# Low-rank products of the RWKV preparations in plain fp32, from a weight tile and an input tile of their own

## The chip, the cores and the metric

The kernel runs on one core of a Trainium2 chip. The metric is device time in microseconds (us) of one execution, the median of the runs shown. Five engines work side by side, each with an instruction queue in order: PE (TensorE, matrix multiply), DVE (VectorE), ACT (ScalarE), POOL (GpSimd) and SP, which here only issues DMA transfers. PEld is PE's loading of weights.

## The reference

One layer of a hybrid decoder on 576 tokens (64 of 8 sampled sequences, 512 of one prompt), width 1024: a joint input projection, a Mamba-2 branch, an RWKV-7 branch, an output projection, a SwiGLU and an embedding gate. The change touches one spot of the RWKV branch, where two low-rank products make the decay and the in-context rate of every token and channel:

```python
u = rw + (prev - rw) * w['shift_mu']          # token shift of the projected columns
r, k, v, w_lo, a_lo, g_lo = jnp.split(u, RWKV_SPLITS, axis=-1)   # w_lo, a_lo: 64 columns each
w_log = -jax.nn.softplus(-(w['w0'] + jnp.tanh(w_lo) @ w['w2']).astype(f32)) - 0.5
decay = jnp.exp(-jnp.exp(w_log))
a = jax.nn.sigmoid((w['a0'] + a_lo @ w['a2']).astype(f32))
```

## The kernel before

Channels lie on the 128 partitions and the 576 tokens along the free axis, in two halves of 288 columns (`HV`). Nearly every matrix product is done to fp32 precision from split operands: a tensor is cast to a high part (type fp32r, on ACT) and the rest is subtracted into a low part (on DVE or POOL), and `mm3` adds up three matmuls, high x high, high x low, low x high. A second helper, `fsum`, multiplies plain fp32 tiles with one matmul instruction a half; before the change it is used for the bonus term only.

Weights stream in blocks of 128 x 512 (`wsplit`, L206 to L213): SP loads a block into `raw` (three buffers), ACT casts it to `whi`, and DVE or POOL makes `wlo`. `whi` and `wlo` have two buffers each, and a buffer is free again when the last matmul that reads it is done. `linear` makes one output tile of 128 channels from two such blocks; a block is 24 matmuls for 576 tokens. A counter, `flip`, is raised by every `split` and `wsplit`; where no engine is named, an odd number gives the low part to POOL and an even one to DVE.

The program begins with the input's normalisation, the projected tile of the low-rank inputs (`ul`: 64 rows for the decay, through tanh, and 64 for the rate) and the tile of the gate. `ul` stays in use until the last quarter; `split` makes `ulh` and `ull` from it, which live in buffers of their own, while `ul` itself is a slot of the shared ring `s`. Meanwhile `norm_x` makes the eight normalised input tiles and their splits `xhi` and `xlo`, and the first projection tiles are computed from the unnormalised input `xu`.

Then the 16 RWKV heads are worked through in four quarters of 256 channels. A quarter has its six projection tiles, the preparation (`prep`: the low-rank products, decays, keys), the Gram matrices (`gram`), the bonus, a triangular solve on DVE (`solve`, `combine`) and a chain over nine chunks of tokens (`chain`). Between these, at places written out by hand (`FP`, `FILL`), `fill` puts further projection tiles (convolution and z) to give PE work. Behind the last quarter come the Mamba-2 branch, the output projection, the SwiGLU with its seven-product scheme (L1424) and the embedding gate.

In a preparation, `wsplit` loads and splits the quarter's low-rank weights `wl` (128 rows: 64 for the decay, 64 for the rate) into one of the two pairs `whi`, `wlo`, and `lora` makes four products from them, two per channel tile, each six matmuls long and read out by a tanh on ACT. `fill_at` may put a projection tile ahead of the first product, between the channel tiles and behind the second (`FP` gives one tile at each of these places in quarters 0 to 2, none in quarter 3).

The order of the instructions on each engine's queue isn't that of the program text. A planner takes instructions by their place in the text as their priority, and by when its own model has them ready and their buffers free, and writes one fixed order per engine.

Of the kernel before, what the change touches and what calls it, by code (L numbers as in the profile page):

```python
# [8 lines left out]
F32 = mybir.dt.float32  # L9
# [7 lines left out]
P = 128  # L17
D = 1024
NT = 576
# [22 lines left out]
RW_LORA, RW_GATE = 24, 25  # L42
# [33 lines left out]
def hybrid_step(ctx, tc, A):  # L76
    nc = tc.nc
# [10 lines left out]
    def nm(s):  # L88
        uid[0] += 1
        return f"{s}_{uid[0]}"  # L90

    def act(out, in_, func=AF.Copy, scale=1.0, bias=0.0):
        return S.activation(out, in_, func, bias=bias, scale=scale)  # L93
# [13 lines left out]
    def lin_ps(off=224):  # L107
        return lin_bank()[:, off:off + NT]
# [19 lines left out]
    def par(name, i=0):  # L128
        at, _ = PV[name]
        return pv[:, at + i:at + i + 1]  # L130
# [54 lines left out]
    def below(lo, src, hi, eng):  # L185

        if eng == "D":
            act(lo, src, scale=-1.0)
            G.dma_start(lo, src, accum_op=ALU.add)
        else:  # L190
            eng.tensor_tensor(lo, src, hi.bitcast(F32), ALU.subtract)  # L191

    def split(src, pool, tags, shape, lo_eng=None, hi=None, lo=None, hi_eng=None, **kw):
        hi = hi if hi is not None else pool.tile(shape, F32R, tag=tags[0], name=nm(tags[0]), **kw)
        lo = lo if lo is not None else pool.tile(shape, F32R, tag=tags[1], name=nm(tags[1]), **kw)
        if hi_eng:
            hi_eng.tensor_copy(hi[:], src)
        else:
            act(hi[:], src)
        flip[0] += 1  # L200
        below(lo[:], src, hi[:], lo_eng or (G if flip[0] % 2 else V))
        return hi, lo

    def wsplit(src, n, hi=None, lo=None):
        raw = wp.tile([P, 512], F32, tag="raw", name=nm("raw"), bufs=3)
        nc.sync.dma_start(raw[:, 0:n], src)  # L206
        if hi is None:
            hi = wp.tile([P, 512], F32R, tag="whi", name=nm("whi"))
            lo = wp.tile([P, 512], F32R, tag="wlo", name=nm("wlo"))
        act(hi[:, 0:n], raw[:, 0:n])  # L210
        flip[0] += 1
        eng = only[0] or (G if flip[0] % 2 else V)
        eng.tensor_tensor(lo[:, 0:n], raw[:, 0:n], hi[:, 0:n].bitcast(F32), ALU.subtract)  # L213
        return hi, lo
# [11 lines left out]
    def mm3(ps, whi, wlo, xhi, xlo, first, last, halves=None):  # L226
        for a, b in halves or HV:
            T.matmul(ps[:, a:b], whi, xhi[:, a:b], start=first, stop=False)  # L228
            T.matmul(ps[:, a:b], whi, xlo[:, a:b], start=False, stop=False)  # L229
            T.matmul(ps[:, a:b], wlo, xhi[:, a:b], start=False, stop=last)  # L230
# [20 lines left out]
    def fsum(ps, w, x):  # L251
        for a, b in HV:
            T.matmul(ps[:, a:b], w, x[:, a:b], start=True, stop=True)
# [3 lines left out]
    sp = mix.enter_context(tc.tile_pool(name="sp", bufs=1, side="right"))  # L257
# [3 lines left out]
    se = early_.enter_context(tc.tile_pool(name="se", bufs=1))  # L261
# [17 lines left out]
    def cb_ps():  # L279
        return bank(sq_, "cb", 1)  # L280

    def slot(name, shape=None, dt=F32):
        return se.tile(shape or [P, NT], dt, tag="s", name=nm(name), bufs=NSLOT)

    def cslot(name, shape=None, dt=F32):
        return sp.tile(shape or [P, NT], dt, tag="cv", name=nm(name), bufs=3)
# [73 lines left out]
            X.append(split(xr[k][:], xp, ("xhi", "xlo"), [P, NT]))  # L360


    def shifted(c, early=False, odd=False):
        ps = lin_ps()
        if early:
            linear(XU, ps)
            u = se.tile([P, NT], F32, tag="ar", name=nm("u"), bufs=2)
            V.tensor_tensor(u[:], ps, r0[:], ALU.mult)
            ps = u[:]
        else:  # L370
            linear(X, ps)
        t = sp.tile([P, NT], F32, tag="vo", name=nm("rw"), bufs=2) if odd else slot("rw")
        act(t[:], ps, AF.Identity, scale=omu[:, c:c + 1])
        mu = par("shift_mu", c)
        V.scalar_tensor_tensor(t[:, 0:65:8], sst[:, c, :], mu, t[:, 0:65:8], ALU.mult, ALU.add)
        V.scalar_tensor_tensor(t[:, ND + 1:NT], ps[:, ND:NT - 1], mu, t[:, ND + 1:NT], ALU.mult, ALU.add)
        t8, p8 = (a[:, 0:ND].rearrange("p (b t) -> p b t", b=8) for a in (t, ps))
        V.scalar_tensor_tensor(t8[:, :, 1:8], p8[:, :, 0:7], mu, t8[:, :, 1:8], ALU.mult, ALU.add)
        act(sho[:, c, 0:8], ps[:, 7:64:8])
        act(sho[:, c, 8:9], ps[:, NT - 1:NT])  # L380
        return t
# [50 lines left out]
        V.scalar_tensor_tensor(x[:], x[:], 0.0, e[:], ALU.max, ALU.add)  # L432
        nc.sync.dma_start(dt_d[:], x[:])

    ul = shifted(RW_LORA, True)
    act(ul[0:64, :], ul[0:64, :], AF.Tanh)
    UL = split(ul[:], se, ("ulh", "ull"), [P, NT], bufs=1)

    def gate_in():
        ug = shifted(RW_GATE, True)  # L440
# [50 lines left out]
    def fill_at(s, i):  # L491
        fill(FP[s.q][i])
# [43 lines left out]
    def prep(s):  # L536
        q = s.q
        mid = q in (1, 2)
        s.AR = (se if mid else sp).tile([P, 2, 9, 64], F32, tag="ar" if mid else "arz", name=nm("ar"), bufs=1 + mid)
        s.G = (se, sp)[q % 2].tile([P, 9, 2, 2, 2, 64], F32, tag=f"G{q % 2}", name=nm("G"))  # L540
        s.PC = sp.tile([P, 2, 16], F32, tag="pc", name=nm("pc"), bufs=2)
        s.BK, s.kn = [], []
        wl = wsplit(A["wl2"][:, q * 512:q * 512 + 512], 512)

        def lora(rows, jj, bias):
            ps = lin_ps()
            c = slice((2 * rows + jj) * P, (2 * rows + jj) * P + P)
            mm3(ps, wl[0][:, c], wl[1][:, c], UL[0], UL[1], True, True)
            t = slot("lo")
            act(t[:], ps, AF.Tanh, scale=0.5, bias=bias)  # L550
            return t

        st = cb_ps()
        for jj in jj2:
            j = 2 * q + jj
            sq = slot("sqk")
            act(sq[:], s.k[jj][:], AF.Square, scale=par("k_k", j))
            token_sums(st, jj, sq)
        fill_at(s, 0)
        rn = inv_norm(st, "rn", 1.0, 0.0)  # L560
        for jj in jj2:
            j = 2 * q + jj
            k, r, v = s.k[jj], s.r[jj], s.v[jj]
            ip = lora(0, jj, hw[:, j:j + 1])
            act(ip[:], ip[:], AF.Identity, scale=0.5, bias=eps_t[:, 2:3])
            a = lora(1, jj, hw[:, 8 + j:9 + j])
            fill_at(s, 1 + 2 * jj)
            V.tensor_tensor_scan(ip[:], rmask[:], ip[:], 0.0, ALU.mult, ALU.add)
            pb = slot("pb", [P, NT + 1])
            act(pb[:, 1:NT + 1], ip[:], AF.Exp, scale=-C_DECAY)  # L570
            act(ip[:], ip[:], AF.Exp, scale=C_DECAY)
            V.tensor_tensor(s.AR[:, jj], g9(r[:]), g9(pb[:, 1:NT + 1]), ALU.mult)
            for e in range(2):
                act(s.G[H[e], :, jj, 1, e], s.AR[H[e], jj])
            G.tensor_copy(s.PC[:, jj, 0:8], pb[:, 8:65:8])
            G.tensor_copy(s.PC[:, jj, 8:16], pb[:, 128:NT + 1:64])
            G.memset(pb[:, 0:65:8], 1.0)
            G.memset(pb[:, 128:NT:64], 1.0)
            kk = slot("kk")
            for a0, b0, ps in by_channel(rn, jj, cb_ps, ""):  # L580
                V.scalar_tensor_tensor(kk[:, a0:b0], k[:, a0:b0], par("k_k", j), ps, ALU.mult, ALU.mult)
            bk = (se, sp)[q % 2].tile([P, 9, 2, 64], F32, tag=f"bk{q % 2}", name=nm("bk"), bufs=2)
            V.tensor_tensor(pb[:, 0:NT], kk[:], pb[:, 0:NT], ALU.mult)
            for e in range(2):
                act(s.G[H[e], :, jj, 0, e], g9(pb[H[e], 0:NT]))
            V.scalar_tensor_tensor(kk[:], a[:], 1.0, kk[:], ALU.add, ALU.mult)
            act(a[:], a[:], AF.Identity, scale=hka[:, j:j + 1], bias=hka[:, 8 + j:9 + j])
            V.tensor_tensor(a[:], a[:], k[:], ALU.mult)
            for e in range(2):
                h = H[e]  # L590
                V.scalar_tensor_tensor(bk[h, :, e, :], g9(kk[h, :]), 0.5, g9(ip[h, :]), ALU.mult, ALU.mult)
                G.tensor_tensor(bk[h, :, 1 - e, :], g9(a[h, :]), g9(ip[h, :]), ALU.mult)
            s.kn.append(a)
            fill_at(s, 2 + 2 * jj)
            s.BK.append(bk)
# [667 lines left out]
    for what in SEQ:  # L1263
# [7 lines left out]
        elif what == "y":  # L1271
            for j in range(6):
                t = cslot("yl")
                nc.sync.dma_start(t[:], yr_d[j][:])
                YR.append(split(t[:], xp, ("xhi", "xlo"), [P, NT], lo_eng=G))
        else:
            ps = lin_ps()
            linear(YR[0:6], ps)
            t = cslot("pr")
# [21 lines left out]
    for c in range(8):  # L1301
        ps = lin_ps()
# [59 lines left out]
    for f in range(3):  # L1362
        ps = lin_ps()
# [18 lines left out]
    for k in range(4):  # L1382
        xa, xb, t = ft("xa"), ft("xb"), ft("tt")
# [13 lines left out]
    for f in range(3, 4):  # L1397
        ps = lin_ps()
# [135 lines left out]
    for a, b in ((0, 320), (320, NT)):  # L1534
# [18 lines left out]
        for c in range(8):  # L1553
# [5 lines left out]
            ps = lin_bank()[:, 0:n]  # L1559
# [8 lines left out]
            t = ft("pg")[:, 0:n]  # L1568
# [8 lines left out]
        ps = rstd_by_token(acc, 1.0 / D, 0, n)  # L1577
# [150 lines left out]
```

## Time and profile before

| | |
|---|---|
| median of 3 runs | 1332.21 us (1329.48 to 1340.11) |
| the profiled execution | 1330.78 us, its span 1328.8 us |
| PE busy | 1225.6 us, 92% of the span |
| DVE, ACT, POOL busy | 887.1, 631.1, 611.6 us |
| mean granted PE clock | 0.95 |

A row of the timeline gives start, duration, engine, line, operation, tiles written and read, shapes, count, and in brackets the time the engine stood idle before it and what ended that. A row of a group gives count, then busy time and mean duration, then idle time before. Matmuls overlap in the records, so the time that one takes of PE is the distance between starts and not its duration. PE's granted clock is 1.00 or 0.50 in any short stretch.

### The profile page before, as it was taken

How to read it: one execution, taken by the hardware profiler on the slowest of the kernel's cores; microseconds unless marked ns; L12 is line 12 of the kernel's file. 1: busy time of each engine (PE TensorE's matmuls, PEld its weight loads, DVE VectorE, ACT ScalarE, POOL GpSimd, SP SyncE). 2: the span in 40 equal slices, each digit the busy share in tenths (PEclk: the TensorE clock that was granted, in tenths of full speed). 3: DMA queues.
4: the chain of work that ended last, by engine and by line, in shares of the span. 5: the costliest groups of instructions: out<-in, count | busy, mean ns of one | idle time of the engine just before them, and what ended most of it. 6: DMA issues, size and time to landing. Idle time of an engine off the chain costs nothing. (4 is left out here: it accounts for less than half of the span.)

```text
span 1328.8 us, 26626 instructions
## 1 busy us (share of the span) xinstructions
PE 1225.6 (92%) x10429; PEld 1127.1 (85%) x10429; DVE 887.1 (67%) x1570; ACT 631.1 (47%) x1274; POOL 611.6 (46%) x583
## 2 busy tenths in 40 slices
PE   6897999999989978899989988999999999999997
PEld 5786897889968966787869868899899999999996
DVE  6648666887696886953456567868895148883464
ACT  6565436534654373343434464455553225553363
POOL 5416513642365135122455655646465345655642
PEclk9898899899978979889989989999999999999998
DMA  5322242234232313262454542253333224424322
GB/s 166 122 69 72 78 116 67 86 96 121 72 110 74 100 52 87 95 200 88 140 187 140 176 151 65 72 169 106 96 107 89 87 76 114 125 57 135 100 88 72
DMA packets 96765, 140.29 MB, mean 106 GB/s; under 512 B 34961, under 2 KB 39313, under 8 KB 96641
## 3 DMA queue, kind: packets, MB, share of 16 engines
q1 hardware_dynamic: 93760, 133.36, 32.8%
q0 software_dynamic: 2304, 4.72, 2.0%
q8 instruction: 82, 1.34, 0.4%
q10 hardware_dynamic: 576, 0.52, 0.1%
q14 instruction: 43, 0.34, 0.1%
HBM read 106.10 MB, written 27.75 MB: 101 GB/s over the span
## 5 line engine op out<-in xcount | busy, mean ns | idle before, releaser
L213 POOL TENSOR_TENSOR wlo<-raw,whi 128x512 fp32r<-128x512 f32 (+1 forms) x92 | 125.4, 1363 | 307.9 <-ACT whi L93 230.3
L228 PE MATMUL lin<-xhi,whi 128*128 128x288 f32 (+1 forms) x784 | 243.0, 311 | 2.9 <-ACT whi L93 2.1
L230 PE MATMUL lin<-xhi,wlo 128*128 128x288 f32 (+1 forms) x784 | 241.2, 308 | 2.2 <-POOL wlo L213 2.2
L229 PE MATMUL lin<-xlo,whi 128*128 128x288 f32 (+1 forms) x784 | 240.8, 307 | 0.9 <-POOL xlo L191 0.9
L93 ACT ACTIVATE whi<-raw 128x512 fp32r<-128x512 f32 (+1 forms) x200 | 123.2, 616 | 213.3 <-PE lin L241 94.9
L228 PEld LDWEIGHTS lin<-xhi,whi 128*128 128x128 f32 (+1 forms) x784 | 150.5, 192 | 9.8 <-ACT whi L93 2.6
L229 PEld LDWEIGHTS lin<-xlo,whi 128*128 128x128 f32 (+1 forms) x784 | 150.3, 192 | 6.2 <-POOL xlo L191 2.1
L230 PEld LDWEIGHTS lin<-xhi,wlo 128*128 128x128 f32 (+1 forms) x784 | 150.3, 192 | 6.0 <-POOL wlo L213 2.8
L213 DVE TENSOR_TENSOR wlo<-raw,whi 128x512 fp32r<-128x512 f32 (+1 forms) x108 | 83.5, 774 | 73.5 <-PE lin L241 37.7
L1424 PE MATMUL lin<-T,wh 128*128 128x288 f32 x576 | 87.3, 296 | 2.6 <-ACT e L93 2.2
L1424 PEld LDWEIGHTS lin<-T,wh 128*128 128x128 f32 x576 | 80.2, 190 | 3.3 <-ACT e L93 2.4
L93 ACT ACTIVATE wh<-raw 128x512 fp32r<-128x512 f32 x72 | 45.1, 629 | 53.9 <-PE lin L1424 37.1
L191 POOL TENSOR_TENSOR wl<-raw,wh 128x512 fp32r<-128x512 f32 x36 | 57.1, 1586 | 13.1 <-PE lin L1424 7.5
L191 DVE TENSOR_TENSOR wl<-sw,wh 128x512 fp32r<-128x512 f32 x54 | 50.8, 940 | 8.6 <-ACT wh L93 4.5
L241 PE MATMUL lin<-ah,whi 128*128 128x288 f32 x352 | 54.7, 294 | 0.0
L241 PE MATMUL lin<-al,whi 128*128 128x288 f32 x352 | 54.4, 295 | 0.0
L241 PE MATMUL lin<-ah,wlo 128*128 128x288 f32 x352 | 54.2, 295 | 0.0
L681 DVE TENSOR_TENSOR tmp<-L,Tt 72x30 f32<-72x30 f32 (+14 forms) x120 | 51.4, 429 | 3.2
L1424 PE MATMUL lin<-T,wl 128*128 128x288 f32 x288 | 50.2, 299 | 0.0
L241 PEld LDWEIGHTS lin<-ah,whi 128*128 128x128 f32 x352 | 49.3, 188 | 0.0
L241 PEld LDWEIGHTS lin<-al,whi 128*128 128x128 f32 x352 | 49.2, 188 | 0.0
L241 PEld LDWEIGHTS lin<-ah,wlo 128*128 128x128 f32 x352 | 49.2, 188 | 0.0
(432 smaller groups left out, 3259.2 us busy)
## 6 DMA issues: line engine op xcount, KB each, us to landing
raw<-wts SPq DMA_DIRECT2D x271, 256.0 KB, 2.6
S<-s_wkv SPq DMA_DIRECT2D x8, 512.0 KB, 5.1
hd<-s_ssm SPq DMA_DIRECT2D x8, 512.0 KB, 3.5
o_ssm_s<-hd SPq DMA_DIRECT2D x8, 512.0 KB, 2.9
xbc_d<-E SPq DMA_DIRECT2D x12, 288.0 KB, 2.1
x<-xT SPq DMA_DIRECT2D x8, 288.0 KB
gate_d<-g SPq DMA_DIRECT2D x8, 288.0 KB, 2.5
bv_d<-rw SPq DMA_DIRECT2D x8, 288.0 KB
```

The costliest lines, as they stand in the source:

```text
L93: return S.activation(out, in_, func, bias=bias, scale=scale)
L191: eng.tensor_tensor(lo, src, hi.bitcast(F32), ALU.subtract)
L213: eng.tensor_tensor(lo[:, 0:n], raw[:, 0:n], hi[:, 0:n].bitcast(F32), ALU.subtract)
L228: T.matmul(ps[:, a:b], whi, xhi[:, a:b], start=first, stop=False)
L229: T.matmul(ps[:, a:b], whi, xlo[:, a:b], start=False, stop=False)
L230: T.matmul(ps[:, a:b], wlo, xhi[:, a:b], start=False, stop=last)
L241: T.matmul(ps[:, a:e], (hi, lo)[p][:, i * P:(i + 1) * P], xs[k + i][q][:, a:e], start=n == k + i == 0, stop=n == 2 and k + i == nk - 1, sk ...
L681: V.tensor_tensor(o, L[:, jx:jx + 1, jx + 1:32].to_broadcast([NB, jx, n]), Tt[:, 0:jx, jx:jx + 1].to_broadcast([NB, jx, n]), ALU.mult)
L1424: T.matmul(ps, (hi, lo)[p][:, k * P:(k + 1) * P], OPS[n][k][q], start=first and p == q == k == 0, stop=p == 1 and k == 3, skip_group_check ...
```

## The change

The low-rank input `ul` gets a buffer of its own of fp32 (in place of `ulh`; `ull` is gone) and isn't split. Each quarter's weights are loaded by SP straight into a tile `wl` of their own (one buffer) and aren't split either. The products are made by `fsum` instead of `mm3`. So the counter `flip` is raised five times less: once before `norm_x` and once in each preparation.

```diff
-    def shifted(c, early=False, odd=False):
+    def shifted(c, early=False, odd=False, home=None):
...
-        t = sp.tile([P, NT], F32, tag="vo", name=nm("rw"), bufs=2) if odd else slot("rw")
+        t = home or (sp.tile([P, NT], F32, tag="vo", name=nm("rw"), bufs=2) if odd else slot("rw"))
...
-    ul = shifted(RW_LORA, True)
+    ul = shifted(RW_LORA, True, home=se.tile([P, NT], F32, tag="ulh", name="ul"))
     act(ul[0:64, :], ul[0:64, :], AF.Tanh)
-    UL = split(ul[:], se, ("ulh", "ull"), [P, NT], bufs=1)
+    UL = ul
...
-        wl = wsplit(A["wl2"][:, q * 512:q * 512 + 512], 512)
+        wl = sp.tile([P, 512], F32, tag="wl", name=nm("wl"), bufs=1)
+        nc.sync.dma_start(wl[:], A["wl2"][:, q * 512:q * 512 + 512])
...
-            mm3(ps, wl[0][:, c], wl[1][:, c], UL[0], UL[1], True, True)
+            fsum(ps, wl[:, c], UL)
```

## The prediction

> **What bounds the kernel now.** I read the page's first parts for the engines, then stages of the span by windows, then the records of the products that change, then PE's waits around them.
>
> ```profile
> span 1328.8 us, 26626 instructions
> PE 1225.6 (92%) x10429; PEld 1127.1 (85%) x10429; DVE 887.1 (67%) x1570; ACT 631.1 (47%) x1274; POOL 611.6 (46%) x583
> 0.00:70.00 70.00, 51.65 (x344) 48.13 (x345) 45.67 (x66) 40.76 (x72) 31.49 (x52) 0.95 0.44 143
> 70.00:110.00 40.00, 36.26 (x285) 34.81 (x284) 22.09 (x36) 26.30 (x47) 11.84 (x13) 0.96 0.20 61
> 110.00:180.00 70.00, 59.59 (x463) 54.50 (x462) 56.20 (x110) 30.22 (x60) 34.46 (x46) 0.85 0.27 79
> 325.00:440.00 115.00, 106.51 (x1050) 93.06 (x1049) 86.19 (x166) 60.03 (x137) 51.67 (x60) 0.90 0.29 89
> 840.00:1200.00 360.00, 351.65 (x2631) 347.24 (x2630) 252.03 (x356) 163.07 (x286) 191.40 (x138) 1.00 0.37 99
> ```
>
> PE is busy 92% of the span and no other engine over 67%. The window rows give the window, its length, then PE, PEld, DVE, ACT and POOL busy time with counts, then the granted clock. From 840 us on PE is full at clock 1.00: what is gained or lost earlier passes to the end one for one. Before that PE stands idle 3.7 us in 70 to 110 and 10.4 us in 110 to 180, and its clock is at times below 1. So the change is worth the PE time that it adds plus the PE gaps that it closes or opens.
>
> **The products.** The first two rows are the reference for plain fp32, the others what goes.
>
> ```profile
> L253 PE MATMUL lin<-lo,blk 128*128 128x288 f32 x32 | 10.6, 460 | 1.1 <-DVE G L638 0.7 <-ACT G L93 0.4
> L908 PE MATMUL cx<-ar,cen 128*128 128x288 f32 x32 | 12.8, 508 | 0.4 <-ACT ar L93 0.4
> L228 PE MATMUL lin<-ulh,whi x32: 291/296/609, 86.2 to 476.0; 128*128 128x288 f32 x32
> L229 PE MATMUL lin<-ull,whi x32: 290/295/446, 86.4 to 476.2; 128*128 128x288 f32 x32
> L230 PE MATMUL lin<-ulh,wlo x32: 288/295/446, 86.5 to 476.3; 128*128 128x288 f32 x32
> L93 ACT ACTIVATE ulh<-rw x1: 683/683/683, 43.6 to 43.6; 128x576 fp32r<-128x576 f32 x1
> L191 POOL TENSOR_TENSOR ull<-rw,ulh x1: 2698/2698/2698, 44.3 to 44.3; 128x576 fp32r<-128x576 f32 x1
> L206 SPq DMA_DIRECT2D raw<-wl x4: 327/328/376, 74.0 to 451.5; - x4
> raw<-wts SPq DMA_DIRECT2D x271, 256.0 KB, 2.6
> ```
>
> There are 16 low-rank products (4 quarters, 2 channel tiles, 2 kinds), each in two halves of 288 columns: 32 halves of three split matmuls now. `fsum`, the helper that the products move to, already runs at L253: 8 bonus products, 16 halves, yet 32 records. A plain fp32 matmul is thus two records a half. Durations overlap, so I take the price from starts:
>
> ```profile
> 315.67 0.29 PE L229 MATMUL lin<-xlo,whi 128*128 128x288 f32 x1
> 315.80 0.65 PE L908 MATMUL cx<-ar,cen 128*128 128x288 f32 x2
> 316.07 0.51 PE L230 MATMUL lin<-xhi,wlo 128*128 128x288 f32 x1
> 316.42 0.29 PE L228 MATMUL lin<-xhi,whi 128*128 128x288 f32 x1
> 316.55 0.65 PE L908 MATMUL cx<-ar,cen 128*128 128x288 f32 x2
> ```
>
> A split matmul starts 0.13 us after the one before (315.67 to 315.80). From 315.80 to 316.55, 0.75 us, PE does two split matmuls (0.27) and one plain half: 0.48 us. A half so goes from 3 x 0.133 = 0.40 to 0.48, and all 32 together cost **+2.7 us** of PE; "one pass" is one instruction in the program, not on PE. Weight loads overlap (PEld 188 ns beside 296) and get fewer. The bounds are +1.3 (the products fall into gaps) and +4.3 (32 x 0.133, if a half cost four split matmuls).
>
> The Trainium skill, FP8 and Floating Point Precision, TensorE Precision Notes, says that true fp32 takes four passes through the array, which speaks against the change: three passes become four. By that rule alone the estimate is that upper bound, +4.3; the trace agrees in direction, with 0.48 us where four split matmuls take 0.53, and the row decides.
>
> **The casts.** Gone are four ACT casts of `wl` weights, their four subtractions, and the cast and subtraction of `ul` (0.68 us on ACT, 2.70 on POOL). I cost these at nothing in themselves: ACT is 47% busy and POOL 46%, and the first product reads `ulh` 43 us after it is made. The cover fails only where an engine queue is what PE waits for, which is the next point. `wl` still takes one load a quarter, now straight to its own tile. It waits for the previous quarter's last product; queued behind it on SP stand the next weight blocks. The four loads are spread over 377 us, so a quarter's products are long done when the next load is issued: nothing, at worst the 0.3 us of an issue. If the first load moves forward to the start and takes the place of a block there, that is bounded by a load's 2.6 us from issue to landing.
>
> **The ring of split weights.** `whi`/`wlo` have two buffers. While a preparation runs, `wl` holds one pair until its last product, so projection tiles between the products have one pair left. ACT and PE of preparation 0:
>
> ```profile
> 82.06 0.63 ACT L93 ACTIVATE whi<-raw 128x512 fp32r<-128x512 f32 x1 [1.33 <-issue]
> 85.20 0.63 ACT L93 ACTIVATE whi<-raw 128x512 fp32r<-128x512 f32 x1 [2.51 <-PE lin L229]
> 98.23 0.63 ACT L93 ACTIVATE whi<-raw 128x512 fp32r<-128x512 f32 x1
> 85.88 0.40 PE L228 MATMUL lin<-xhi,whi 128*128 128x288 f32 x1 [0.47 <-ACT whi L93]
> 98.92 0.53 PE L228 MATMUL lin<-xhi,whi 128*128 128x288 f32 x1 [1.67 <-ACT whi L93]
> 106.83 0.40 PE L230 MATMUL lin<-xhi,wlo 128*128 128x288 f32 x1 [0.82 <-POOL wlo L213]
> 232.20 0.61 PE L230 MATMUL lin<-xhi,wlo 128*128 128x288 f32 x1 [1.09 <-POOL wlo L213]
> 95.00:99.00 4.00, 1.55 (x12) 1.13 (x10) 1.86 (x5) 3.90 (x9) 0.92 (x4) 1.00 0.00 0
> 99.00:102.40 3.40, 3.40 (x13) 3.09 (x14) 3.37 (x5) 3.33 (x6) 0.90 (x2) 0.50 0.27 81
> ```
>
> The cast at 82.06 is `wl`; the one at 85.20 waited for PE to free the other pair, and PE waited 0.47 us for it. At 98.92 PE waited 1.67 us for a block cast late, and the gap is followed by 3.4 us at clock 0.50, in which 13 matmuls ran instead of 25: 12 x 0.133 = 1.6 us lost. With a second pair free the 98.23 cast can be a block ahead, before ACT's crowd of 95 to 99 (busy 3.90 of 4.00). Gain **-3.7 us**. Bounds: nothing, if ACT's chain ends last there anyway (PE then waits for the next elementwise step); -5.6, if the waits for a low part at 106.83 and, behind preparation 1, at 232.20 go too. Preparation 3 has no fillers to gain from it.
>
> **The alternation.** Each split takes the next number of a counter, odd to POOL, even to DVE. Five numbers vanish, so the engines swap from `ul` to preparation 0, between preparations 1 and 2, and from preparation 3 to the end. In full stages a block is 3.2 us of PE and either engine is in time. At the start it shows:
>
> ```profile
> 29.73 2.27 DVE L359 SCALAR_TENSOR_TENSOR x<-x,pv,rstd 128x576 f32<-128x576 f32 x3
> 32.58 6.67 DVE L359 SCALAR_TENSOR_TENSOR x<-x,pv,rstd 128x576 f32<-128x576 f32 x5
> 33.58 0.61 ACT L93 ACTIVATE whi<-raw 128x512 fp32r<-128x512 f32 x1
> 34.27 1.73 POOL L213 TENSOR_TENSOR wlo<-raw,whi 128x512 fp32r<-128x512 f32 x1 [0.76 <-ACT whi L93]
> 45.06 0.68 DVE L213 TENSOR_TENSOR wlo<-raw,whi 128x512 fp32r<-128x512 f32 x1
> 45.80 0.61 PE L230 MATMUL lin<-xu,wlo 128*128 128x288 f32 x1 [5.45 <-DVE wlo L213]
> 44.40:51.20 6.80, 5.40 (x22) 5.40 (x23) 5.68 (x9) 2.60 (x6) 5.69 (x3) 0.50 0.29 81
> ```
>
> PE stood 5.45 us for a low part that DVE came to only at 45.06. That block goes to POOL, and the block before it (cast 33.58, needed 24 x 0.133 = 3.2 us before 40.35, near 37) from POOL to DVE, behind the five normalisations that last till 39.25. So the stall goes and another comes a block earlier, until 40 at the earliest and 45 at the latest. Behind it stand 46 matmuls, 28 of them in the 6.8 us at half clock that follow such a stall and 18 at full (2.4): the tile ends between 49.2 and 54.2, now at 51.2. That is -2 to +3; I take **0**, near the middle. The best case, DVE taking the block at once, is -8 (the 5.45, and 2.5 for 23 matmuls at half clock).
>
> The five normalisations took 1.33 us each beside POOL's work, three before them 0.76 each. The Trainium skill, SBUF — State Buffer, Who interferes with whom, says that a DVE instruction with two SBUF inputs contends with a GpSimd instruction that reads SBUF; these rows agree. Two more of the eight input splits fall to POOL here, so by it the start would lean to the late end, +3.
>
> **Sum.** +2.7 - 3.7 + 0 = -1.0 us. The profiled execution took 1330.78 us, 2.0 beyond its span, and lies 1.4 under the median 1332.21. So 1329.8 in its terms, 1331 as a median. About 1% (13 us) is what a measurement of this kernel can tell from no change.
>
> **Rivals.**
> *The start comes out well.* Start -8, preparations -5.6, products +2.7: -10.9, some 1321. For it: POOL is idle when the swapped block needs it. Against: DVE's queue is long just when the other block needs it.
>
> *PE's clock falls in the solve stage: slower.* The instruction order is planned anew, and with a pair free projection tiles move into the preparation and are missing behind it, where PE fills its gaps with them:
>
> ```profile
> 122.90:140.00 17.10, 11.62 (x74) 9.71 (x72) 11.25 (x18) 7.45 (x18) 14.35 (x19) 0.50 0.09 23
> 382.30:402.80 20.50, 17.69 (x165) 14.53 (x167) 16.12 (x33) 10.93 (x29) 6.57 (x12) 0.50 0.27 96
> ```
>
> These stretches already run at half clock. One more as long as the second, with PE as full, costs half its 20.5 us, 10; with +2.7 and the late start +3 that is +16: 1347. It decides where idle of 2 to 3 us, like that before 98.92, is opened anew behind a preparation. Against it: the number of fillers per place is written out by hand and unchanged.
>
> *The change doesn't do what it says.* If the plan still lets casts come as late as now, only the price of the products stays: +2.7, 1335, within the forecast's own range.
>
> **How the numbers follow.** Forecast with the third rival, 1324 to 1342: 0.62. The good start: 0.18, of which over half stays within 1%. The lost clock: 0.20, most of it beyond 1%. Faster by over 1% then has 0.10, within 1% 0.70, slower 0.20. The range takes the good start with some reordering beyond it and reaches to the lost clock: 1317 to 1347.
>
> **What would show it.** 64 records of plain fp32 for the products in place of 96, about 0.24 us apart at full clock; no cast onto `ulh` and no `ull`; PE's waits for `whi` at 86 and 99 gone and clock 1.00 behind them; PE's stall for a low part near 37 instead of 46; PE busy up by some 2 to 3 us. Wrong would be: span off by over 13 us, with a new half-clock stretch between 110 and 500, or the input stall gone altogether.

## The result and the profile after

The changed kernel takes 1354.73 us (median of 4 runs, 1354.53 to 1358.08) against 1332.03 us for the kernel before, measured beside it (1329.48 to 1340.11): ratio **1.0152**, 95% interval 1.0113 to 1.0192. It is slower by 1.5%, and outside the forecast range of 1317 to 1347. The profiled execution took 1354.83 us.

The first lines of the page after, and the same windows as before (window, length, busy time of PE, PEld, DVE, ACT, POOL, granted clock, DMA share, GB/s):

```profile
span 1353.0 us, 26553 instructions
PE 1245.1 (92%) x10397; PEld 1139.0 (84%) x10397; DVE 875.9 (65%) x1567; ACT 628.8 (46%) x1267; POOL 603.7 (45%) x581
```

```profile
0.00:70.00 70.00, 48.29 (x323) 44.78 (x324) 44.39 (x62) 38.68 (x68) 29.77 (x52) 0.93 0.44 143
70.00:110.00 40.00, 37.09 (x293) 35.45 (x292) 20.23 (x36) 23.51 (x46) 9.58 (x16) 0.98 0.27 76
110.00:180.00 70.00, 59.86 (x423) 53.49 (x422) 54.67 (x103) 31.79 (x59) 32.16 (x41) 0.77 0.24 67
325.00:440.00 115.00, 104.84 (x1022) 90.15 (x1021) 76.95 (x158) 60.08 (x135) 50.77 (x59) 0.92 0.34 95
840.00:1200.00 360.00, 352.78 (x2654) 347.97 (x2651) 247.12 (x351) 162.77 (x282) 195.39 (x138) 1.00 0.38 104
```

DVE, ACT and POOL did less than before, and PE has 32 matmuls fewer, yet PE was busy 19.5 us longer. From 840 us on it runs at full clock as before. So the loss lies ahead of that, and it is largely clock: 0.77 in place of 0.85 between 110 and 180.

A split of the span shows this for all kernels. **PE idle** is the span less PE's busy time. **Clock lost** is half of PE's busy time inside the stretches at clock 0.50. What remains is **PE work** at full clock. Before: 103.2 + 54.6 + 1171.0. After: 107.9 + 72.5 + 1172.5. Of the 24.2 us, 4.7 are idle, 17.9 clock and 1.5 work.

By stage, idle and clock lost together grow most where two preparations end: from quarter 1's first tanh behind a product to its first solve row by 7.2 us (11.3 to 18.5), and in quarter 3 by 9.0 (17.2 to 26.2). Behind that they grow by another 2.5 to the end (60.5 to 63.0). The windows of these two stages, first before, then after:

```profile
211.20:276.50 65.30, 60.32 (x526) 49.75 (x526) 49.37 (x84) 39.21 (x87) 41.31 (x52) 0.90 0.28 83
471.20:530.90 59.70, 47.63 (x571) 36.01 (x570) 43.36 (x82) 32.92 (x77) 31.24 (x35) 0.89 0.22 63
481.30:495.00 13.70, 10.25 (x103) 8.44 (x95) 11.47 (x19) 9.28 (x18) 4.63 (x6) 0.50 0.07 24
```

```profile
220.40:290.00 69.60, 59.77 (x514) 48.11 (x514) 49.80 (x87) 37.62 (x85) 37.81 (x52) 0.85 0.29 83
488.70:551.60 62.90, 51.52 (x452) 38.54 (x446) 40.28 (x73) 29.23 (x68) 26.69 (x32) 0.73 0.16 46
497.50:511.20 13.70, 9.69 (x49) 5.75 (x49) 11.68 (x16) 8.50 (x16) 7.31 (x8) 0.50 0.00 1
514.60:518.00 3.40, 1.11 (x6) 0.39 (x4) 3.39 (x4) 2.84 (x7) 1.68 (x2) 1.00 0.54 162
518.00:538.50 20.50, 19.93 (x196) 17.48 (x198) 9.07 (x25) 6.57 (x20) 6.20 (x9) 0.50 0.15 52
```

Quarter 3 had one stretch of 13.7 us at half clock; now it has that and a second of 20.5 us, in which PE is busy for 19.93 us. Half of that, 10 us, is lost. PE's waits ahead of the second stretch, after:

```profile
512.33 1.07 PE L857 MATMUL cx<-um,bkt 128*64 128x512 f32 x2 [0.90 <-POOL um L854]
516.15 0.29 PE L805 MATMUL cx<-xs,TT 64*64 64x64 f32 x2 [1.10 <-DVE S L859]
518.57 0.58 PE L805 MATMUL cx<-xs,TT 64*64 64x64 f32 x5 [1.75 <-DVE xs L800]
```

Short waits of the chain (`cx`) stand right ahead of it, with PE busy 1.11 of 3.4 us. Once the clock is down, six windows of 3.4 us pass before it returns, though PE's records are nearly gapless. The matmuls do run at half speed there: those of L797 start 213 ns apart (median), against 112 ns at full clock. The Trainium skill, TensorE: Matmul & The Clock Gate, What's actually happening, gives a window of about 3.4 us, an idle one halving the clock and a busy one restoring it. The length agrees, since the stretches here are multiples of 3.4; the fall came behind a window that was idle for two thirds only; the return doesn't agree, as 97% busy by the records kept 0.50 for 20.5 us.

### The profile page after: what moved, and what is told of

Same layout as the page of the kernel before. It is cut to its first block, busy times and chain, and to the rows that moved or that the text cites. A ratio compares the mean times of both kernels' runs of the same rounds, so it can differ in the third digit from the quotient of the medians.

```text
span 1353.0 us, 26553 instructions
## 1 busy us (share of the span) xinstructions
PE 1245.1 (92%) x10397; PEld 1139.0 (84%) x10397; DVE 875.9 (65%) x1567; ACT 628.8 (46%) x1267; POOL 603.7 (45%) x581
## 5 line engine op out<-in xcount | busy, mean ns | idle before, releaser
L213 POOL TENSOR_TENSOR wlo<-raw,whi 128x512 fp32r<-128x512 f32 (+1 forms) x90 | 117.6, 1307 | 309.5 <-ACT whi L93 249.5
L230 PE MATMUL lin<-xhi,wlo 128*128 128x288 f32 (+1 forms) x784 | 244.0, 312 | 0.0
L593 POOL TENSOR_TENSOR bk<-lo,lo 64x576 f32<-64x576 f32 x16 | 28.3, 1770 | 48.3 <-DVE lo L589 47.7
```

## The experiments

Four theories were set against each other. **P**: the loss is the order that the planner writes anew. **F**: fp32 products cost more than thought. **C**: the counter `flip`. **R**: the pair freed in the ring of split weights lets a block go ahead of the products. (**K**, in the expectations of e5 to e8, says that the missing casts move the order; it is P by another way than R.) The likeness below is counted from the built programs: the largest share of PE's matmuls, the low-rank products left out, that stand in the same sequence in both (1.00: the same order). The expectations use a coarser count of their own, 0.81 for e10 and 0.80 for e2.

| run | ratio, 95% interval | PE order's likeness to before | PE idle, clock lost, PE work (us) |
|---|---|---|---|
| the change | 1.0152 [1.0113, 1.0192] | 0.89 | 107.9, 72.5, 1172.5 |
| e1 change, old order | 0.9985 [0.9964, 1.0006] | 1.00 | 100.7, 58.0, 1176.1 |
| e2 change, counter kept | 1.0163 [1.0125, 1.0200] | 0.88 | 117.7, 63.5, 1177.1 |
| e3 counter alone | 1.0052 [1.0022, 1.0082] | 0.91 | 108.5, 58.2, 1171.6 |
| e4 fp32 products alone | 1.0004 [0.9983, 1.0025] | 0.95 | 98.8, 59.2, 1176.8 |
| e5 ring freed alone | 1.0060 [1.0038, 1.0082] | 0.93 | 100.7, 65.5, 1170.8 |
| e6 change, ring held | 1.0128 [1.0091, 1.0165] | 0.94 | 110.4, 66.7, 1176.4 |
| e7 change, tiles behind | 1.0007 [0.9986, 1.0028] | 0.94 | 107.4, 54.4, 1174.8 |
| e8 change, tiles far behind | 1.0055 [1.0027, 1.0083] | 0.92 | 110.0, 56.9, 1178.8 |
| e9 change, PE's old order | 0.9983 [0.9962, 1.0003] | 1.00 | 101.2, 56.2, 1173.5 |
| e10 before, one slot more | 1.0108 [1.0083, 1.0133] | 0.93 | 109.5, 65.5, 1169.7 |
| e11 before, tiles behind | 1.0240 [1.0214, 1.0266] | 0.89 | 117.7, 75.3, 1172.7 |
| e12 change as it is, tiles behind | 1.0015 [0.9995, 1.0035] | 0.92 | 104.7, 60.9, 1171.4 |
| e13 old order until quarter 2 | 1.0027 [1.0007, 1.0046] | 0.98 | 102.0, 58.5, 1172.8 |
| e14 old order from quarter 2 | 0.9990 [0.9973, 1.0007] | 0.96 | 100.0, 59.5, 1172.5 |
| e15 old order until quarter 3 | 0.9979 [0.9955, 1.0004] | 0.99 | 99.9, 62.3, 1174.1 |
| e16 old order from quarter 3 | 1.0036 [1.0013, 1.0059] | 0.94 | 109.1, 54.9, 1175.6 |
| e17 before, PE's new order | 1.0409 [1.0384, 1.0434] | 0.88 | 128.8, 82.1, 1172.4 |
| e18 the same, own pair | 1.0298 [1.0266, 1.0329] | 0.88 | 125.0, 79.4, 1169.2 |

The last column is of one profiled execution each; executions of one kernel differ by several us, so the ratios decide.

**The order, the counter, the products.** Every instruction of an engine is tied to the one ahead of it in the old order, with no semaphore. In e1 all engines but POOL are tied; POOL comes out the same but for one swap of neighbours (casts and low parts of weights not counted).

```diff
+def pinned(tc):
...
+        for a, b in zip(order, order[1:]):
+            tc.add_manual_dep(traced[b], traced[a].name,
+                              mybir.DependencyInfo(mybir.DependencyClass.NoSync, mybir.DependencyReason.DATA),
+                              reason="pinned")
...
             hybrid_step(ctx, tc, A)
+            pinned(tc)
```

In e1 and e2 the counter is stepped on where a split is gone; e3 steps it back in the kernel before:

```diff
     UL = ul
+    flip[0] += 1
...
         nc.sync.dma_start(wl[:], A["wl2"][:, q * 512:q * 512 + 512])
+        flip[0] += 1
```

In e4 the kernel before multiplies the high parts alone by `fsum`; the low parts' products are left out, the casts stay:

```diff
-            mm3(ps, wl[0][:, c], wl[1][:, c], UL[0], UL[1], True, True)
+            fsum(ps, wl[0][:, c].bitcast(F32), UL[0].bitcast(F32))
```

> The whole change (plain fp32 products, own buffers, no casts), but every engine but POOL is held to the order that the kernel before issues its instructions in, and the counter that deals low parts to POOL and DVE is stepped on as before. If the loss is the new order (theory P), this takes 1332 plus the products' price of 0 to 3 us: 1329 to 1336. If the products themselves cost what was lost (theory F: plain fp32 is dearer than its starts show, or keeps the clock low), it takes some 1350 to 1357. If it is the swapped counter (theory C), it takes 1332 too, and the next two runs tell C from P.

> The change with the counter stepped on by hand in the five places, so that each low part is made by the engine that made it before; the order is planned anew. Theory C: 1332 to 1336. Theories P and F: still 1345 to 1357, less some 4 us if the input stall near 40 us is the counter's.

> The kernel before with the counter stepped back in the same five places, so that low parts swap between POOL and DVE as in the change, and nothing else. Theory C: the whole loss, 1350 to 1357. Theories P and F: 1332 to 1342, of which some 4 us are the longer input stall (9 us in place of 5.5) and its half clock.

> The kernel before with the 16 low-rank products as one plain fp32 matmul a half, read from the high parts as they are (the low parts of weights and input are left out of the products); the casts, the ring of split weights that they hold and the counter stay. Theory F: 1350 to 1357. Theory P: the order is planned anew because products take longer, so anything from 1330 to 1350; if the loss comes from the freed ring of split weights, 1332 to 1338.

With the counter kept the whole loss stays (1.0163), and with the old order on top it is gone (0.9985): the same operations, 1334.5 or 1357.3 us. The products alone cost nothing that shows (1.0004). So F falls, as e1 has the fp32 products and no loss; C cost 0.5% on the kernel before and isn't needed for the change's loss; and P stands. The stage from quarter 3's products to its solve, in e1 and then in e2:

```profile
474.60:532.90 58.30, 48.02 (x571) 36.11 (x570) 44.07 (x87) 31.41 (x75) 31.23 (x35) 0.88 0.21 64
```

```profile
481.80:545.20 63.40, 55.81 (x500) 41.11 (x500) 37.49 (x76) 30.54 (x70) 26.89 (x32) 0.75 0.16 45
```

With the old order PE issues 571 matmuls there at clock 0.88, as before (571 at 0.89); in the new one 500 at 0.75.

**The ring.** e5 gives the split pair of `wl` buffers of its own in the kernel before. e6 has the change take a pair of the ring at each preparation's start, with a memset of one column, and release it behind the last product, with an addition of zero:

```diff
-        wl = wsplit(A["wl2"][:, q * 512:q * 512 + 512], 512)
+        wl = wsplit(A["wl2"][:, q * 512:q * 512 + 512], 512, *(sp.tile([P, 512], F32R, tag=f"wl{p}", name=nm("wl"), bufs=1) for p in "hl"))
```

```diff
+        held = [wp.tile([P, 512], F32R, tag=t, name=nm(t)) for t in ("whi", "wlo")]
+        for t in held:
+            G.memset(t[:, 0:1].bitcast(F32), 0.0)
...
+            for t in held if jj else ():
+                G.tensor_tensor(a[:, 0:1], a[:, 0:1], t[:, 0:1].bitcast(F32), ALU.add)
```

> The kernel before, split products and all casts and the counter as they are, but the split low-rank weights lie in a pair of buffers of their own and no longer in the ring of projection weights. Theory R (the freed ring lets the planner put one more block of 24 projection matmuls ahead of a quarter's products, 3.2 us of PE, and that late preparation is paid for in the solve and the chain): 1348 to 1360. Theory K (the missing casts and subtractions move the order): 1330 to 1340.

> The change with the counter kept (1357 with the ring free), and a pair of the projection weights' buffers taken at the start of each preparation and given back behind its last product, as the split weights had it; two small memsets and two additions of zero on POOL a quarter do it. Theory R: 1332 to 1340. Theory K: 1350 to 1360.

Freeing the ring alone costs 0.6%, which lies between what the two theories gave it; holding it leaves 1.3% of the 1.6% of e2. Each of these two has a new order throughout, so the plainer evidence is e1 and e9 (below), where the ring is free and nothing is lost. The ring is one way to a new order, and not the cause. R falls as the whole.

**Where the projection tiles stand.** In PE's order the change's plan has 410, 960 and 1488 projection matmuls ahead of the first products of quarters 0 to 2, where before had 386, 936 and 1464: a block of 24 more each time. It is the freed ring that moves them: e5 has 410, 960 and 1488 as well, and e6, with the ring held, is back at 386, 936 and 1464 and still loses 1.3%. e7, e8 (the change with the counter kept), e12 (the change as it is) and e11 (before) move tiles behind the products; e8 has `(0, 0, 0, 1, 2, 0, 0, 0)`:

```diff
-FP = ((1, 0, 1, 0, 1, 0, 0, 0), (1, 0, 1, 0, 1, 0, 0, 0), (1, 0, 1, 0, 1, 0, 0, 0), (0, 0, 0, 0, 0, 0, 0, 3))
+FP = ((0, 1, 0, 1, 1, 0, 0, 0), (0, 1, 0, 1, 1, 0, 0, 0), (0, 1, 0, 1, 1, 0, 0, 0), (0, 0, 0, 0, 0, 0, 0, 3))
```

> The change with the counter kept and the ring free, but the two projection tiles that stand ahead of the products in the preparation's text stand behind the two products of each channel tile. Theory R: the products come first again, 1325 to 1338, and the free pair may show a gain over the kernel before. Theory K: 1350 to 1360.

> As the run before, but one tile behind the last product and two at the preparation's end. Theory R: the products come still earlier, but fewer tiles cover the elementwise steps between them: 1325 to 1345. Theory K: 1350 to 1360.

> Before, with the projection tiles of quarters 0 to 2 placed behind the products as in the run that brought the change back to 1.0007, and nothing else. If the change's loss came from its tiles going ahead of the products, that placement helps the change alone: here 0.998 to 1.008 (before has no such loss, and a tile placed late may open a gap). If the placement is simply a better one, worth 1.5% to any kernel, and the change's loss is untouched beneath it: 0.983 to 0.990 here.

> The change as it is, its counter not kept, with the projection tiles of quarters 0 to 2 behind the products. The tiles' place has cured the loss with the counter kept (1.0007); the counter alone cost 0.5% on before. If the two add up: 1.004 to 1.008, with PE's stall of about 9 us for a low part near 46 us. If the placement works only in one plan by luck: over 1.010. Faster than 0.996 would make it the version to keep.

For the change the move pays (1.0007, and 1.0015 where 1.004 to 1.008 was expected), which looked like the cause found. But the same move makes the kernel before 2.4% slower, more than either expectation allowed. So the number of tiles ahead of the products isn't what decides: each of these edits has the whole order written anew, and each order comes out differently.

**The order by itself.** e9 ties PE alone. e10 changes `NSLOT` from 10 to 11: the ring `s` of the preparations gets one slot more, and no operation comes or goes. The change touches this ring at one place, since its `ul` no longer takes a slot there; e10 gives room of the same kind, and its waits for a slot can differ too. e17 is the kernel before with PE tied to e2's order, and e18 adds e5's buffers:

```diff
-NSLOT = 10
+NSLOT = 11
```

> The change with its counter kept, as in the run that cost 1.6%, but PE alone issues in the order that it had before; the planner places the other engines' instructions around it (their orders then come out 0.96 to 0.98 like before's by themselves). P (the loss is in PE's order of projection tiles against the chain): ratio 0.997 to 1.004, and the stretch from quarter 3's products to its solve loses 5 to 6 us to half clock. If the loss sits in another engine's order (DVE's or ACT's places for the casts, chain and solve): 1.008 to 1.016, 15 us lost there.

> Before, with 11 slots in place of 10 for the preparations' tiles and nothing else: no operation comes or goes, but the planner writes another order (PE's is 0.81 like before's, as far from it as the change's 0.80). If any other order costs as much as the change's did (the order before is a lucky one): 1.005 to 1.016. If the change's plan is worse than most for a reason of its own (its freed buffers or missing casts): 0.997 to 1.004 here.

> The kernel before with all its operations (split products, casts, the ring of two); PE alone issues in the order that the planner wrote for the change with the counter kept (ratio 1.0163 there). If the order by itself is the loss: 1.012 to 1.020, with 12 us or more lost to half clock from quarter 3's products to its solve. If the order costs only together with what the change does (fp32 products, casts gone): 0.998 to 1.005.

> The same, with the split low-rank weights in buffers of their own, so that projection tiles never wait for that pair. If the order by itself is the loss: as the run beside it, 1.012 to 1.020. If the run beside it is slower only because its ring holds the tiles up in an order made for a free ring: 1.00 to 1.006 here.

PE's old order is enough (0.9983); the other engines then come out near their old orders by themselves. A replan with every operation of before kept costs 1.1%, though its order is nearer to before's (0.93) than the change's is (0.89). And e2's order for PE slows the old operations by 4.1%, 3.0% with the ring freed, both more than the 1.2 to 2.0% expected. The same stage of quarter 3 in e9, then in e10, then in e17:

```profile
469.60:529.50 59.90, 49.14 (x566) 37.20 (x565) 41.80 (x82) 32.42 (x76) 30.16 (x34) 0.86 0.20 59
```

```profile
476.20:539.10 62.90, 49.63 (x515) 37.33 (x514) 40.97 (x74) 29.55 (x66) 29.04 (x35) 0.76 0.20 60
```

```profile
507.60:571.40 63.80, 55.98 (x506) 42.01 (x505) 38.84 (x77) 31.55 (x72) 27.58 (x33) 0.73 0.17 48
```

The clock of this stage goes with the order (0.86, 0.76, 0.73) and not with the operations: e10 and e17 have the old ones, e9 the new. Within e2's order for PE the change is the faster kernel: 1.0163 against 1.0409. The step from e17 to e18 (0.011) is the ring, the rest casts, products, the slot of `ul` and the other engines' orders together, which these runs don't part. In the old order that gain doesn't show (0.9983, 0.9985).

**Which part of the order.** PE is tied to the old order only up to, or only from, the first product of quarter 2 or 3; the rest is planned.

```diff
+ORDER = {"PE": old order[:k]}   # e13, e15; old order[k:] in e14, e16
```

> The change with its counter kept; PE issues in the order of before up to quarter 2's first low-rank product, and in the planner's order behind it. If the loss is set up early (the blocks of tiles ahead of the products of quarters 0 and 1): 0.997 to 1.004. If each stage makes its own: the stages from there on lost about 15 of the 27 us in the run with the whole new order, so 1.006 to 1.012.

> The reverse: the planner's order up to quarter 2's first product, PE's order of before from there on. If the loss is set up early: 1.010 to 1.016. If each stage makes its own: 1.003 to 1.009, with the stretch from quarter 3's products to its solve back at 5 to 7 us of half clock lost.

> PE in the order of before up to quarter 3's first product, the planner's order behind it. If the loss is set up earlier: 0.997 to 1.004. If the planner's order in quarter 3's stage and behind it is what loses 10 us of clock: 1.005 to 1.010, with 10 us or more lost to half clock from quarter 3's products to its solve.

> The planner's order up to quarter 3's first product, PE's order of before from there on. If the loss is set up earlier: 1.010 to 1.016, as with the whole new order. If quarter 3's stage makes a third of it by itself: 1.006 to 1.011, with 5 to 7 us lost to half clock from its products to its solve in place of 15.

Both expectations of e14, and of e16, are missed on the low side, and no part shows the loss: 1.0027 and 0.9990, 0.9979 and 1.0036, where the whole is 1.0163. What was tested differs, though. In e14 and e16 the planned part is e2's: up to the product its matmuls stand in e2's sequence (1.00 of them). So e2's order up to quarter 3's first product costs 0.4% when before's order follows (e16), and most of e2's loss needs e2's order behind that product. In e13 and e15 the planned part isn't e2's: it is 0.97 and 0.98 like before's, where e2's own is 0.89 and 0.91. So e2's late order behind before's early one was not tried.

The profiled executions fit. From quarter 3's first tanh to the end, idle and clock lost are 77.7 us in before, 97.3 in e2 and 81.2 in e16; ahead of it they are 80.2, 84.1 and 82.8. Quarter 3's stage in e16, where PE again has before's order:

```profile
475.96:537.32 61.36, 50.07 (x576) 37.86 (x577) 44.97 (x86) 32.55 (x78) 30.57 (x34) 0.89 0.21 64
```

In the change itself the loss is shared: 91.3 us ahead of that tanh and 89.1 behind it. **Open** is what in the order does it: the runs name a stretch of e2, not a wait. e2 also loses more of it as idle (117.7 against 103.2 us) than as clock, the change more as clock. That short waits of the chain behind quarter 3's preparation are followed by a half-clock stretch is seen in the trace; that they are the whole of it was not shown.

No version beats the kernel before. The change with PE's order held, wholly (e9, 0.9983) or up to quarter 3 (e15, 0.9979), comes nearest, and both intervals contain 1.

## Why the prediction was wrong

**The sum's total fits where the order is held; the order was not held.** All terms were priced as if the rest of the program stayed where it was. With the order held, and the counter kept, the change comes out near the sum: -1.0 us forecast, -2.0 (e1, 0.15% of 1335) and -2.3 (e9) measured, with 2.8 us on either side. That is too wide to confirm the single terms, and the ring's came out smaller (below). The step that failed is what the sum left out: the new plan had no term of its own and stood only as a rival of chance 0.20. It is worth some +23 us (1357.25 against 1334.48, e2 and e1).

**The slower rival** was what came, and its size was near: 1347 forecast, 1354.7 measured. It named one more half-clock stretch as long as that of 20.5 us, costing 10; the trace has such a stretch, of that length, in quarter 3. The idle ahead of it, 2.29 of 3.4 us, is of the size that the rival gave. The change also lost 7 us more in quarter 1, which the rival didn't have. Its reason was wrong: the freed pair does move a block of tiles ahead of the products, but in quarters 0 to 2 and not in quarter 3, by itself it costs 0.6% (e5), and the loss stays without it (e6). That the size came near is in part luck. And the argument against it, that the number of fillers per place is written out by hand and unchanged, carried no weight: with that number and every operation unchanged e10 loses 1.1%.

**The products** were right. The change has the 64 records. Their group, and PE's rows around the first of them:

```profile
L253 PE MATMUL lin<-ul,wl x64: 403/406/848, 91.3 to 492.8; 128*128 128x288 f32 x64
```

```profile
91.33 1.13 PE L253 MATMUL lin<-ul,wl 128*128 128x288 f32 x4
92.09 0.51 PE L230 MATMUL lin<-xhi,wlo 128*128 128x288 f32 x1
92.44 0.30 PE L228 MATMUL lin<-xhi,whi 128*128 128x288 f32 x1
```

From 91.33 to 92.44, 1.11 us, PE does two halves and one split matmul (0.13): 0.49 us a half, 0.48 forecast. PE's work is 1174.8 us on average in the thirteen kernels with fp32 products and 1171.1 in the seven with split ones: +3.7, for +2.7 within bounds of 1.3 and 4.3. Single profiles scatter more than that (1171.4 to 1178.8 and 1169.2 to 1172.7).

**The casts** at nothing: no gain or loss shows. e1 has none of them in the old order (0.9985), and e4, which keeps them all but has an order of its own, is level with it (1.0004, overlapping intervals).

**The ring of split weights** gave what was forecast at its place, and it was taken back a few us on. ACT's casts, PE's windows and PE's next waits in the change:

```profile
87.88 0.63 ACT L93 ACTIVATE whi<-raw 128x512 fp32r<-128x512 f32 x1 [2.54 <-PE lin L229]
91.18 0.63 ACT L93 ACTIVATE whi<-raw 128x512 fp32r<-128x512 f32 x1
96.80 0.63 ACT L93 ACTIVATE whi<-raw 128x512 fp32r<-128x512 f32 x1 [1.25 <-issue]
```

```profile
86.00:92.00 6.00, 6.00 (x45) 5.89 (x44) 2.18 (x6) 3.58 (x7) 1.29 (x1) 1.00 0.33 86
95.00:99.00 4.00, 3.84 (x25) 3.31 (x26) 1.46 (x5) 2.72 (x6) 1.49 (x3) 1.00 0.00 0
99.00:102.40 3.40, 3.40 (x29) 3.40 (x28) 0.89 (x2) 3.33 (x7) 1.14 (x5) 1.00 0.36 88
108.40:118.60 10.20, 7.89 (x27) 6.77 (x28) 10.05 (x11) 6.42 (x11) 4.50 (x5) 0.50 0.23 66
```

```profile
109.01 2.29 PE L253 MATMUL lin<-ul,wl 128*128 128x288 f32 x4 [2.75 <-ACT E L93]
113.00 0.61 PE L228 MATMUL lin<-xhi,whi 128*128 128x288 f32 x1 [1.70 <-ACT lo L93]
```

The casts come early, the waits at 86 and 99 are gone, and the clock is 1.00 behind them. Then PE's next products wait 2.75 us for ACT's `E`, and 10.2 us at half clock follow in place of 3.4: 7.89 us of busy time, so 3.9 lost where 1.7 were. From the first tanh to the first solve row, idle and clock lost are 22.9 us before and 25.5 after. That is the bound "nothing, if ACT's chain ends last there anyway", and a little worse. With the old order (e9) PE's wait there is also for `E`, 1.98 us:

```profile
99.37 1.24 PE L253 MATMUL lin<-ul,wl 128*128 128x288 f32 x4 [1.98 <-ACT E L93]
```

The half-clock stretch behind it stays away in e1 and e9 (clock 1.00 from 95 to 102.4), and up to the first solve row they lose 0.9 and 1.8 us less than before. Of the 3.7 forecast that is at most half: this one stretch went, as forecast, and the idle stayed (13.7 us before, 13.3 and 14.0 in e1 and e9).

**The alternation** came out at its late end. DVE's rows and PE's wait at the start, after:

```profile
32.61 6.60 DVE L359 SCALAR_TENSOR_TENSOR x<-x,pv,rstd 128x576 f32<-128x576 f32 x5
39.13 1.37 DVE L375 SCALAR_TENSOR_TENSOR ul<-sst,pv,ul 128x9 f32<-128x9 f32 x1
42.16 1.41 DVE L378 SCALAR_TENSOR_TENSOR ul<-u,pv,ul 128x56 f32<-128x56 f32 x1
45.15 0.68 DVE L213 TENSOR_TENSOR wlo<-raw,whi 128x512 fp32r<-128x512 f32 x1
```

```profile
45.88 0.61 PE L230 MATMUL lin<-xu,wlo 128*128 128x288 f32 x1 [9.04 <-DVE wlo L213]
```

"45 at the latest" was 45.15, behind the three steps of `ul` that now follow the normalisations, and PE stood 9.04 us in place of 5.45. The first product's tanh is 4.1 us later (92.5 against 88.4), a little beyond the bound of +3 where 0 was taken. With the counter kept this is gone, yet e2 is no faster than the change: the gain at the start doesn't show beside what the order loses behind it. On before, the counter costs 0.5% (e3), again with an order written anew.

## What to carry to other kernels

Where a planner writes the instruction order, an edit has two prices: what its operations cost in the old order, and what the new order costs. Measure them apart, by tying the changed kernel to the old order and by an edit that replans and does nothing else. Here the first was 0 and the second 1.5 to 1.8%, and until the order is held, a part tried alone tells little of the part: the eleven kernels with an order wholly planned anew (the change, e2 to e8, e10 to e12) ranged from 1.0004 to 1.024 and none was faster. So part of the loss is that the order of before is a good one among those that this planner writes. And where an order is tied in part, count what the untied part became before reading the result.

## What the runs showed that was not expected

The size of the planner's scatter: an eleventh slot in a ring cost 1.1% (1.0108), and moving tiles cured one kernel (1.0163 to 1.0007) and cost the other 2.4%.

The clock's hold on a chain of small matmuls: 196 matmuls in 20.5 us with PE 19.93 us busy by its records stayed at 0.50 throughout, so here busy by the records didn't bring the clock back.

The two orders and the two sets of operations don't pair evenly: before's operations lose 4.1% in PE's order planned for the change, while the change loses nothing in the order planned for before.
